# A hybrid decoder layer: the mixer's gates taken out of the pair loop into a second pass of seven-product blocks

## The chip, the core and the metric

The kernel runs on one core of a Trainium2 chip. The metric is device time in microseconds (us) of one execution; three runs of the kernel before gave 1593.44 us in the median (1592.82 to 1595.67). A profile is one further execution, recorded by the hardware profiler.

## What is computed

One decoder layer on x of 1024 tokens x 1024 channels, in float32. Cut to what matters:

```python
h = rms_norm(x, norm_mix)
xa, ga, q, f, v, g, m_a, m_b = split(h @ w_in)          # eight projections, 1024 x 1024 each
xa = causal_depthwise_conv(xa)
r, i = sigmoid(xa @ w_r + b_r), sigmoid(xa @ w_i + b_i)  # blocks of 256 channels
log_a = -8 * r * softplus(-lam)
hh = scan(exp(log_a), sqrt(-expm1(2 * log_a)) * (i * xa))   # linear recurrence over tokens
y_a = hh * gelu(ga)
o = rms_norm(hgrn2(silu(q), f_gate(f), v), hg_norm)         # 8 heads of 128, decayed linear attention
y = sigmoid(m_a) * y_a + sigmoid(m_b) * o * silu(g)
x = x + y @ w_out
x = x + square(relu(rms_norm(x, norm_mlp) @ w_up)) @ w_down
return rms_norm(x, norm_final)
```

## The kernel before

Every product is taken in three passes: an operand is split into a rounded high part (H, a cast on ScalarE, line 78) and the rest (L, a subtraction on VectorE, line 79), and `mm3` (lines 123 to 125) issues H x H, H x L and L x H into one PSUM bank. "One matmul" below is one of these three. The engines are called TensorE (PE), VectorE (DVE, `V` in the code), ScalarE (ACT, `A`), GpSimd (POOL, `G`) and SyncE (SP, whose queue issues nearly all DMAs in program order).

The tokens are worked in two halves c of T = 512. For each half, `first_norm(c)` normalizes four tiles of 128 rows, transposes them on TensorE and splits them into `hT`. Then come four pairs p of 256 channels (two heads, one rg block). A pair projects v (`project_v`), xa, q and f (`project_steps`: 8 steps of 6 matmuls of 128x512, 48 in all), convolves xa (`conv`), runs the gated recurrence (`rg_lru`, 24 matmuls, scheduled ahead by a raised priority, placed after the second step of f), and then the attention (`hgrn`). `hgrn` is a long chain on VectorE and ScalarE with small blocks of scores between (tiles `sc`, then `pk`, `pkv`, `po`). While that chain runs, TensorE works on the generator `gates`: the four projections g, mb, ga, ma of the same pair, 48 matmuls each, with their activations. `go(GO[i])` says how many of the generator's steps are issued before each block of scores; GO = (17, 5, 1, 1, 2). The pair's y goes, split, into SBUF. TensorE's instructions are kept in the order in which they are written (`pin`); the other engines' instructions are placed by the scheduler, each engine then running its own in order.

Between the halves stands `out_proj(0)` with `first_norm(1)` in its middle. After the second half comes `out_proj` of the second half, into which the second norm (`second_norm`) is woven, and then the MLP. The MLP uses a product of 2x2 blocks with seven products in place of eight: `PLAN` names, for each of the seven steps, a PSUM bank (X, Y or Z), a combination of weight blocks (A11, A12, A22, s1 to s4, made by `quad_steps`) and a combination of the four blocks of the activation (B11, B21, B22, t1, n2, T3, T4, made by `combos`). One such block of work is 84 matmuls of 128x512. Sixteen blocks are the up projection (uX, uY, uZ in the trace), sixteen the down projection (dX, dY, dZ).

Weight tiles come in `seq` order: `load_w` into one of 4 raw buffers (0.5 MB), `split_w` into two of 6 split buffers. `next_w` takes the next one and fills up to two ahead.

Of the kernel before, what the change touches and what calls it, by code (L numbers as in the profile page):

```python
# [18 lines left out]
P = 128  # L19
# [9 lines left out]
ORDER = ("v", "xa", "q", "f0", "rg", "f1", "g", "mb", "ga", "ma")  # L29
N_PAIR_TILES = 17  # L30
# [4 lines left out]
GO = (17, 5, 1, 1, 2)  # L35
# [8 lines left out]
def trunk(ctx: ExitStack, tc: tile.TileContext, x, wts, mlp, pv, gains, mask_f, mask_u, out):  # L44
# [12 lines left out]
    a2y, close_y = opened("a2y")  # L57
    a2h, close_h = opened("a2h")
# [5 lines left out]
    seq = []  # L64
    for c in range(NC):
        seq += list(range(MIX_TILES + OUT_TILES))
    seq += list(range(MIX_TILES, MIX_TILES + OUT_TILES))
# [16 lines left out]
    def load_w(i):  # L84
        raw = raw_tile(f"raw{i}")
        nc.sync.dma_start(raw, wts[i])
        return raw
# [10 lines left out]
    def fill_w(n):  # L98
        while made[0] < min(n, len(seq)):
            i = seq[made[0]]  # L100
# [48 lines left out]
    def transposed(xn, dst, tt, name):  # L149
        for h in range(2):  # L150
            pt = bank("hg", f"xT_{name}_{h}")
            for k in range(4):
                PE.transpose(pt[:, k * P : (k + 1) * P], xn[:, (4 * h + k) * P : (4 * h + k + 1) * P], ident)
# [3 lines left out]
    def a2_set(pool, name):  # L157
        return [
            [pool.tile([P, 4, T], F32R, tag="a2", name=f"{name}{q}{h}", bufs=4) for h in range(2)] for q in ("H", "L")
        ]  # L160
# [4 lines left out]
    xt_cm = tc.tile_pool(name="xt", bufs=2)  # L165
    xt_pool = xt_cm.__enter__()

    def tile_x(name):
        return xt_pool.tile([P, D], F32, tag="xt", name=name)

    x2d = [dram.tile([P, D], F32, tag=f"x2_{t}", name=f"x2_{t}") for t in range(8)]
# [3 lines left out]
    mix = tc.tile_pool(name="mix", bufs=1)  # L175
# [8 lines left out]
    def small_inputs():  # L184
        nc.sync.dma_start(pvt, pv)
        nc.sync.dma_start(mf, mask_f)
        mu32 = mt("kT", "mu32", (P, 4, P)).rearrange("p a b -> p (a b)")[:, : 7 * 32]
# [9 lines left out]
    t3, t4, t5, t6 = (par[:, i, :] for i in range(3, 7))  # L197

    def parameters():
# [27 lines left out]
        V.tensor_scalar(sp4, t3, 4.0, None, op0=ALU.mult)  # L227

# [10 lines left out]
    hT = []  # L239

    X_TAGS = ("g1", "g2", "on", "xc")

    def first_norm(c):
        dst = a2_set(a2h, f"hT{c}")
        xts = []
        for tt in range(4):
            r = c * 4 + tt
            xt = mt(X_TAGS[tt], f"x{r}", (P, D)) if c == 0 else tile_x(f"x{r}")
            nc.sync.dma_start(xt, x[r * P : (r + 1) * P, :])
            xts.append(xt)  # L250
            if c == 0 and tt == 0:
                gain0.append(gain_tile(0))
            if c == 0 and tt < 3:
                raws.append(load_w(seq[tt]))
        xns = {}

        def rows(tt):
            xns[tt] = mt("f" if tt % 2 == 0 else "tmp", f"xn{c}{tt}", (P, D))
            norm_rows(xts[tt], xns[tt], gain0[0], f"x{c}{tt}")

        def weights(n):
            if c == 0:
                fill_w(n)

        rows(0)
        weights(1)
        transposed(xns[0], dst, 0, f"x{c}0")
        rows(1)
        weights(2)
        for tt in range(1, 4):  # L270
            if tt < 3:
                rows(tt + 1)
            transposed(xns[tt], dst, tt, f"x{c}{tt}")
        weights(3)
        in_order[0] = False
        hT.append(dst)

    def project_steps(c, name):

        pp = [bank("pj", f"pj_{name}_{s}") for s in range(2)]  # L280
        for half in range(2):
            wh, wl = next_w()
            for k in range(4):
# [4 lines left out]
                yield  # L288
# [11 lines left out]
    def project(c, name):  # L300
        return run(project_steps(c, name))

    def project_v(c, name):
        v = mt("v", f"v_{name}", (P, 4, 256))
        w = [next_w(), next_w()]
        for tt in range(4):
            pp = bank("pj", f"pv_{name}_{tt}")
            for k in range(8):
# [4 lines left out]
                mm3(pp[:, :256], hh[:, cut], hl[:, cut], wh[:, cols], wl[:, cols], k == 0, k == 7)  # L313
            A.copy(v[:, tt, :], pp[:, :256])  # L314
        return v

    def conv(c, p, pp):
        xc = mt("xc", f"xc{c}{p}", (P, 2, T))
        for s in range(2):
            u = 2 * p + s  # L320
            xp = mt("xp", f"xp{c}{u}", (P, T + 16), bufs=2)
            V.tensor_copy(xp[:, 0:3], xcar[:, u, :])
# [7 lines left out]
            )  # L330
            for j in range(3):
# [15 lines left out]
    def rg_lru(c, p, xc, xh, xl):  # L347
        wh, wl = next_w()
        hs = mt("h", f"h{c}{p}", (P, 2, T))
        for s in range(2):  # L350
# [6 lines left out]
            w = mt("rw", f"rw{c}{u}")  # L357
            A.activation(w, pr, AF.Sigmoid, bias=pvt[:, PV_BR + u : PV_BR + u + 1])
            A.activation(w, w, AF.Tanh, scale=sp4[:, u : u + 1])
            ig = mt("ri", f"ri{c}{u}")  # L360
            A.activation(ig, pi, AF.Sigmoid, bias=pvt[:, PV_BI + u : PV_BI + u + 1])

            V.tensor_scalar(w, w, 0.0, None, op0=ALU.max)
            rec = mt("rr", f"rr{c}{u}")
            V.tensor_scalar(rec, w, 1.0, None, op0=ALU.add)
            V.reciprocal(rec, rec)  # L366
            A.activation(w, w, AF.Sqrt)
            V.tensor_tensor(out=ig, in0=ig, in1=xc[:, s, :], op=ALU.mult)
            V.scalar_tensor_tensor(w, w, 2.0, rec, op0=ALU.mult, op1=ALU.mult)
            V.tensor_tensor(out=ig, in0=ig, in1=w, op=ALU.mult)  # L370
            V.tensor_scalar(rec, rec, 2.0, -1.0, op0=ALU.mult, op1=ALU.add)
            h = hs[:, s, :]
            V.tensor_tensor_scan(h, rec, ig, hcar[:, u : u + 1], op0=ALU.mult, op1=ALU.add)
            if c + 1 < NC:
                G.tensor_copy(hcar[:, u : u + 1], h[:, T - 1 : T])
        return hs
# [25 lines left out]
    def hgrn(c, p, q1, f, kk, v, go):  # L402
# [90 lines left out]
        go(GO[0] - (OWN_BEFORE if c > 0 else 0))  # L493
# [71 lines left out]
        vn = lambda s, n: v[:, n, s * P : (s + 1) * P]  # L565
# [5 lines left out]
        kT = []  # L571
        for s, u in both:
            kT.append(mt(("kT", "rr")[s], f"kT{c}{u}", (P, 4, P)))
# [6 lines left out]
        states = []  # L580
        for s, u in both:
            sn = mt(("rw", "ri")[s], f"sn{c}{u}", (P, 4, P))
# [38 lines left out]
        return on  # L621

    def gates(c, p, got, dst):
        pg = yield from project_steps(c, f"g{c}{p}")
        g2 = mt("g2", f"g2{c}{p}", (P, 2, T))
        for s in range(2):
            A.activation(g2[:, s, :], pg[s], AF.Sigmoid)
            V.tensor_tensor(out=g2[:, s, :], in0=g2[:, s, :], in1=pg[s], op=ALU.mult)
        pb = yield from project_steps(c, f"mb{c}{p}")
        t = mt("tmp", f"smb{c}{p}", (P, 2, T))  # L630
        for s in range(2):
            A.activation(t[:, s, :], pb[s], AF.Sigmoid)  # L632
        V.tensor_tensor(out=g2, in0=g2, in1=t, op=ALU.mult)
        pa = yield from project_steps(c, f"ga{c}{p}")
        g1 = mt("g1", f"g1{c}{p}", (P, 2, T))
        t = mt("tmp", f"gel{c}{p}", (P, 2, T))
        for s in range(2):
            A.activation(t[:, s, :], pa[s], AF.Square)
            A.copy(g1[:, s, :], pa[s])
        V.tensor_scalar(t, t, 0.044715, 1.0, op0=ALU.mult, op1=ALU.add)  # L640
        V.tensor_tensor(out=t, in0=t, in1=g1, op=ALU.mult)
        A.activation(t, t, AF.Tanh, scale=GELU_C)
        V.scalar_tensor_tensor(g1, t, 1.0, g1, op0=ALU.add, op1=ALU.mult)
        pm = yield from project_steps(c, f"ma{c}{p}")
        for s in range(2):
            pt = bank("hg", f"poT{c}{p}{s}")
            for n in range(4):
                pin(PE.transpose(pt[:, n * P : (n + 1) * P], got["on"][:, 4 * s + n, :], ident))
            V.scalar_tensor_tensor(
                g2[:, s, :], pt, pvt[:, PV_HG : PV_HG + 1], g2[:, s, :], op0=ALU.mult, op1=ALU.mult  # L650
            )
        t = mt("tmp", f"sma{c}{p}", (P, 2, T))
        for s in range(2):
            A.activation(t[:, s, :], pm[s], AF.Sigmoid)
        V.scalar_tensor_tensor(g1, g1, 0.5, got["h"], op0=ALU.mult, op1=ALU.mult)
        for s in range(2):
            V.tensor_tensor(out=t[:, s, :], in0=g1[:, s, :], in1=t[:, s, :], op=ALU.mult)
            V.tensor_tensor(out=t[:, s, :], in0=t[:, s, :], in1=g2[:, s, :], op=ALU.add)
            split(t[:, s, :], *kt(dst, 2 * p + s))

    def out_proj(c, ys, res, done, between=lambda: None):
        for hf in range(2):
            pp = [bank("pj", f"po{c}{hf}{tt}") for tt in range(4)]
            for j in range(4):
                wh, wl = next_w()
                for k in range(2):
                    ku = 2 * j + k
                    yh, yl = kt(ys, ku)
# [8 lines left out]
            if hf == 0:  # L677
                between()

    def res0(tt, hf):  # L680
        xs = xt_pool.tile([P, 512], F32, tag="xs", name=f"xs{tt}{hf}", bufs=2)
# [6 lines left out]
    for c in range(NC):  # L688
        if c == 0:
            first_norm(0)  # L690
            mu32 = small_inputs()
        else:
            out_proj(0, ys, res0, done0, lambda: first_norm(1))
        ys = a2_set(a2y, f"y{c}")
# [20 lines left out]
    xt_cm.__exit__(None, None, None)  # L715
    close_h()

# [393 lines left out]
```

## Time and profile before

| | before |
|---|---|
| median of three runs | 1593.44 us (1592.82 to 1595.67) |
| the profiled execution | 1595.84 us, of which the span is 1594.0 us |
| PE busy | 1560.2 us, 98% of the span |
| DVE busy | 1206.5 us, 76% |
| ACT busy | 771.6 us, 48% |
| POOL busy | 64.9 us, 4% |
| granted TensorE clock, mean | 0.996 |
| moved by DMA | 246.51 MB, 155 GB/s in the mean |

The span runs from the first instruction to the last, and an engine's busy time is the part of it in which an instruction of its own runs. A matmul's duration in a row is longer than the distance to the next one, since they are pipelined. In rows of groups, `out<-in` gives the tiles' names with their numbers left out, then shapes, the count, busy time and mean ns, and after the last bar the idle time just before and what ended it. In rows of waits stand the waiting engine, tile and line, the releaser, and then total us, times and the longest. In rows of single instructions the start in us comes first, then the duration.

### The profile page before, as it was taken

How to read it: one execution, taken by the hardware profiler on the slowest of the kernel's cores; microseconds unless marked ns; L12 is line 12 of the kernel's file. 1: busy time of each engine (PE TensorE's matmuls, PEld its weight loads, DVE VectorE, ACT ScalarE, POOL GpSimd, SP SyncE). 2: the span in 40 equal slices, each digit the busy share in tenths (PEclk: the TensorE clock that was granted, in tenths of full speed). 3: DMA queues.
4: the chain of work that ended last, by engine and by line, in shares of the span. 5: the costliest groups of instructions: out<-in, count | busy, mean ns of one | idle time of the engine just before them, and what ended most of it. 6: DMA issues, size and time to landing. Idle time of an engine off the chain costs nothing.

```text
span 1594.0 us, 23215 instructions
## 1 busy us (share of the span) xinstructions
PE 1560.2 (98%) x9240; PEld 1305.6 (82%) x9240; DVE 1206.5 (76%) x1751; ACT 771.6 (48%) x1210; POOL 64.9 (4%) x107
## 2 busy tenths in 40 slices
PE   7999999999999999999999988999999999999997
PEld 6888898888888888888888866888888878888886
DVE  5985966958754865858759787988877888888877
ACT  4643545446433544546445576777667732221113
POOL 0010010100100010000100100000000000000000
PEclk9999999999999999999999998999999999999999
DMA  6212213222243213222222452766666565666652
GB/s 240 94 67 95 95 64 106 91 83 85 88 171 133 93 67 104 82 80 93 80 93 93 146 198 79 286 242 241 255 254 251 224 265 228 251 250 255 257 200 106
DMA packets 57996, 246.51 MB, mean 155 GB/s; under 512 B 6688, under 2 KB 6816, under 8 KB 47136
## 3 DMA queue, kind: packets, MB, share of 16 engines
q1 hardware_dynamic: 56304, 239.27, 40.3%
q10 hardware_dynamic: 1584, 5.77, 1.0%
q8 instruction: 72, 1.18, 0.3%
q14 instruction: 36, 0.29, 0.1%
HBM read 185.24 MB, written 59.77 MB: 154 GB/s over the span
## 4 chain that ended last, share of the span: by engine, by line
PE 66%; DVE 4%; DMA 1%; ACT 1%; issue 1%; POOL 0%; DVEq 0%; POOLq 0%; SPq 0%; ACTq 0%
PE dX L123 3%; PE uX L123 3%; PE dX L124 3%; PE dX L125 3%; PE uX L125 3%; PE uX L124 3%; PE uY L124 2%; PE uY L123 2%; PE uY L125 2%; PE po L124 2%; PE po L123 2%; PE po L125 2%; PE dY L123 2%; PE dY L124 2%; PE dY L125 2%; PE pj_ma L125 1%
## 5 line engine op out<-in xcount | busy, mean ns | idle before, releaser
L79 DVE TENSOR_TENSOR wL<-raw,wH 128x1024 fp32r<-128x1024 f32 x160 | 194.9, 1218 | 141.6 <-ACT wH L78 140.0
L78 ACT CAST wH<-raw 128x1024 fp32r<-128x1024 f32 x160 | 167.6, 1048 | 117.4 <-PE po L124 27.3
L1031 DVE TENSOR_TENSOR acc<-acc,dX 128x512 f32<-128x512 f32 x128 | 85.0, 683 | 29.4 <-PE dX L125 28.8
L78 ACT CAST wA<-q 128x512 fp32r<-128x512 f32 x32 | 19.8, 622 | 133.1 <-PE dX L125 101.5
L1031 DVE TENSOR_TENSOR acc<-acc,dY 128x512 f32<-128x512 f32 x64 | 43.4, 685 | 15.7 <-PE dY L125 14.5
L366 DVE RECIPROCAL rr<-rr 128x512 f32<-128x512 f32 x16 | 53.5, 3345 | 0.0
L891 ACT ACTIVATE b<-b 128x512 f32<-128x512 f32 x48 | 30.2, 630 | 37.1 <-DVE b L890 37.1
L123 PE MATMUL pv<-wH,hT0H 128*128 128x256 f32 x128 | 37.1, 290 | 0.2 <-ACT wH L78 0.2
L124 PE MATMUL pv<-wL,hT0H 128*128 128x256 f32 x128 | 36.7, 287 | 0.0
L125 PE MATMUL pv<-wH,hT0L 128*128 128x256 f32 x128 | 36.7, 287 | 0.0
L123 PE MATMUL pv<-wH,hT1H 128*128 128x256 f32 x128 | 36.5, 285 | 0.0
L124 PE MATMUL pv<-wL,hT1H 128*128 128x256 f32 x128 | 36.2, 283 | 0.0
L125 PE MATMUL pv<-wH,hT1L 128*128 128x256 f32 x128 | 36.2, 283 | 0.0
L332 DVE SCALAR_TENSOR_TENSOR xc<-xp,pvt,xc 128x512 f32<-128x512 f32 x48 | 33.1, 745 | 0.0
L892 ACT ACTIVATE b<-b 128x512 f32<-128x512 f32 x48 | 30.0, 630 | 1.1
L79 DVE TENSOR_TENSOR wA<-q,wA 128x512 fp32r<-128x512 f32 x32 | 22.0, 687 | 10.6 <-ACT wA L78 10.0
L511 ACT COPY kk<-kc 128x512 f32<-128x512 f32 x8 | 5.0, 622 | 45.1 <-DVE kc L405 45.1
L518 POOL TENSOR_SCALAR scT<-dd 32x256 f32<-32x256 f32 x32 | 23.1, 721 | 78.2 <-DVE dd L434 76.7
L123 PE MATMUL pj_ga<-hT1H,wH 128*128 128x512 f32 x64 | 26.2, 410 | 0.0
L123 PE MATMUL pj_ga<-hT0H,wH 128*128 128x512 f32 x64 | 26.2, 409 | 0.0
L314 ACT COPY v<-pv 128x256 f32<-128x256 f32 x32 | 11.8, 370 | 29.5 <-PE pv L125 29.5
L632 ACT ACTIVATE smb<-pj_mb 128x512 f32<-128x512 f32 x16 | 9.6, 599 | 34.1 <-PE pj_mb L125 34.1
(1861 smaller groups left out, 5252.4 us busy)
## 6 DMA issues: line engine op xcount, KB each, us to landing
raw<-wts_in SPq DMA_DIRECT2D x160, 512.0 KB, 3.4
q<-mlp_in SPq DMA_DIRECT2D x64, 512.0 KB, 4.0
x<-x_in SPq DMA_DIRECT2D x8, 512.0 KB, 6.4
acc<-x ACTq DMA_DIRECT2D x8, 512.0 KB, 6.3
y_out<-acc SPq DMA_DIRECT2D x16, 256.0 KB, 2.0
xs<-x_in SPq DMA_DIRECT2D x8, 256.0 KB, 3.4
x<-xs SPq DMA_DIRECT2D x8, 256.0 KB, 2.4
x2s<-x_in SPq DMA_DIRECT2D x4, 512.0 KB, 4.5
```

Source lines behind the costliest of these rows:

```text
L78: keep(A.copy(h, src))
L79: keep(V.tensor_tensor(out=lo, in0=src, in1=h.bitcast(F32), op=ALU.subtract))
L123: pin(PE.matmul(o, ah, bh, start=first, stop=False, **how))
L124: pin(PE.matmul(o, ah, bl, start=False, stop=False, **how))
L125: pin(PE.matmul(o, al, bh, start=False, stop=last, **how))
L314: A.copy(v[:, tt, :], pp[:, :256])
L332: V.scalar_tensor_tensor(xc[:, s, :], xp[:, j : j + T], pvt[:, PV_CW + 8 * j + u : PV_CW + 8 * j + u + 1], xc[:, s, :], op0=ALU.mult, op1= ...
L366: V.reciprocal(rec, rec)
L518: G.tensor_scalar(scT[32 * b : 32 * b + 32, :, 32 * b : 32 * b + 32], dd[32 * b : 32 * b + 32, :, :], 1.0, 0.0, op0=ALU.mult, op1=ALU.add,)
L891: A.activation(b[:, at, :], b[:, at, :], AF.Relu, scale=-1.0 if at == 2 else 1.0)
L892: A.activation(b[:, at, :], b[:, at, :], AF.Square)
L1031: V.tensor_tensor(out=dst, in0=dst, in1=banks[bk, pr], op=op)
```

## The change

The mixer is worked in two passes.

**Pass 1** runs over the eight (half, pair) items i. `hgrn(i)` is issued with a generator beside it as before, but the generator is now `stage(i + 1)`: v of item i, transposes of `on` of item i - 1 (`on_T`), then xa, the convolution, q, f and `rg_lru` of item i + 1. The h of the recurrence and the transposed `on` are written to memory (`hd`, `od`). The four row tiles of the second half are loaded, normalized and transposed inside the first four stages (`next_rows`). `rg_lru` takes its decay from an Exp on ScalarE instead of a reciprocal on VectorE, works on both 512-channel halves in one instruction where it can, and its ScalarE operations are chained in an order by hand. `make_combos(k)`, eight rounds written after the rg gate of stages 5 to 7, makes t1, n2, T3 and T4 of `hT` (six sums on POOL, two on VectorE, four splits) and writes them to memory (`cd`). The last stage projects v of the last item and g and mb of pair 0 plainly.

**Pass 2** computes the other 14 of 16 gate projections over both halves at once, each as one block of seven products (`gate_step`, 84 matmuls), with the gates' arithmetic in `gate_work`. It reads t1, n2, T4 and T3 back (eight loads of 1 MB), h and `on` pair by pair, and writes y, split, to memory. Then `out_proj(0)` and the rest follow as before.

```diff
-GO = (17, 5, 1, 1, 2)
+GO = (24, 5, 1, 1, 2)
...
+    def make_combos(i):
+        k, cut = i // 2, slice(256 * (i % 2), 256 * (i % 2) + 256)
+        r = tile_x(f"r{i}").rearrange("p (a b) -> p a b", a=4)
+        quarters = ((0, 0), (0, 1), (1, 1), (1, 0))
+        for j, (c, h) in enumerate(quarters):
+            hi, lo = (hT[c][q][h][:, k, cut].bitcast(F32) for q in range(2))
+            G.tensor_tensor(out=r[:, j, :], in0=hi, in1=lo, op=ALU.add)
+        b11, b21, b22, b12 = (r[:, j, :] for j in range(4))
+        G.tensor_tensor(out=b11, in0=b11, in1=b12, op=ALU.subtract)
+        G.tensor_tensor(out=b12, in0=b22, in1=b12, op=ALU.subtract)
+        V.scalar_tensor_tensor(b22, b11, -1.0, b22, op0=ALU.mult, op1=ALU.subtract)
+        V.scalar_tensor_tensor(b21, b22, -1.0, b21, op0=ALU.mult, op1=ALU.subtract)
+        for src, o in ((b11, "t1"), (b22, "n2"), (b12, "T3"), (b21, "T4")):
...
+            split(src, st[:, at, 0, :].bitcast(F32R), st[:, at, 1, :].bitcast(F32R))
+            nc.sync.dma_start(cd[o][:, :, k, cut], st[:, at])
...
-            rec = mt("rr", f"rr{c}{u}")
-            V.tensor_scalar(rec, w, 1.0, None, op0=ALU.add)
-            V.reciprocal(rec, rec)
-            A.activation(w, w, AF.Sqrt)
...
+        for s, u in us:
+            on_act(e[:, s, :], w[:, s, :], AF.Exp, scale=nsp8[:, u : u + 1])
+        for s, u in us:
+            on_act(w[:, s, :], w[:, s, :], AF.Tanh, scale=sp4[:, u : u + 1])
+        V.tensor_tensor(out=ig, in0=ig, in1=xc, op=ALU.mult)
+        V.tensor_scalar(w, w, 0.0, None, op0=ALU.max)
+        V.scalar_tensor_tensor(xc, e, 1.0, w, op0=ALU.add, op1=ALU.mult)
+        on_act(w, w, AF.Sqrt)
+        V.tensor_scalar(xc, xc, -1.0, 1.0, op0=ALU.mult, op1=ALU.add)
+        V.scalar_tensor_tensor(w, e, 1.0, w, op0=ALU.add, op1=ALU.mult)
+        V.tensor_tensor(out=ig, in0=ig, in1=w, op=ALU.mult)
...
+        nc.sync.dma_start(hd[p][:, 2 * c : 2 * c + 2, :], hs)
...
-        go(GO[0] - (OWN_BEFORE if c > 0 else 0))
+        go(GO[0] - 8 * (c + p == 0) - (OWN_BEFORE if c > 0 else 0))
...
+    def v_of(i):
+        def between(tt):
+            if tt == 0 and i > 1:
+                on_T(*where(i - 2), gots[i - 2])
+            if tt == 1 and "xn" in gots[i - 1]:
+                transposed(gots[i - 1]["xn"], hT[1], i - 1, f"x1{i - 1}")
+
+        yield from v_steps(*where(i - 1), gots[i - 1], between)
+
+    def stage(i):
+        c, p = where(i)
+        got = gots[i]
+        if i == 0:
+            yield from v_steps(c, p, got, lambda tt: None)
+        elif i > 1:
+            yield from v_of(i)
+        px = yield from project_steps(c, f"xa{c}{p}")
+        xc, xps = conv_in(c, p, px)
...
+        pq = yield from hooked(project_steps(c, f"q{c}{p}"), {} if i == 1 else {6: convolve})
+        got["q1"] = q_of(c, p, pq)
+        yield
+        fs = hooked(project_steps(c, f"f{c}{p}"), {6: convolve} if i == 1 else {})
+        for _ in range(2 if i != 1 else 7):
+            next(fs)
+            yield
...
+        yield from rg_lru(c, p, *got["xc"])
+        if i < 4:
+            got["xn"] = next_rows(i)
+        for k in {5: (0, 1, 2), 6: (3, 4, 5), 7: (6, 7)}.get(i, ()):
+            make_combos(k)
+        if i != 1:
+            pf = yield from fs
+            got["f"], got["kk"] = f_of(c, p, pf)
...
+    def last_stage():
+        yield from v_of(NC * NPAIR)
...
+        on_T(NC - 1, NPAIR - 1, gots[-1])
...
+    for i in range(NC * NPAIR):
+        rest = stage(i + 1) if i + 1 < NC * NPAIR else last_stage()
+        hgrn(*where(i), gots[i], lambda n: run(rest, n))
+        run(rest)
...
+    for o in ("t1", "n2", "T4", "T3"):
+        pool = np_ if o in ("t1", "n2") else tp
+        gop[o] = tuple(pool.tile([P, 4, T], F32R, tag=o + q, name=f"g{o}{q}") for q in "HL")
+        for q in range(2):
+            nc.sync.dma_start(gop[o][q].bitcast(F32), cd[o][:, q])
...
+    def gate_step(q, step):
+        bk, wo, ho = PLAN[step]
...
+        for k in range(4):
+            cols = slice(k * P, (k + 1) * P)
+            mm3(o, wh[:, cols], wl[:, cols], hh[:, k, :], hl[:, k, :], first and k == 0, k == 3, not first)
+        if step < 3:
+            ge[q, step] = gp.tile([P, T], F32, tag="e", name=f"ge{step}_{q}", bufs=4)
+            A.copy(ge[q, step], o)
+        elif step < 6:
+            at, e = {3: (0, 0), 4: (2, 1), 5: (3, 2)}[step]
+            V.tensor_tensor(out=b[:, at, :], in0=o, in1=ge.pop((q, e)), op=ALU.add)
+        else:
+            A.copy(b[:, 1, :], o)
...
+    own = list(range(2, QUADS))
+    for q in own[:2]:
+        load_quad(GQ + q)
+        gwork[q] = quad_steps(GQ + q, (w1p, wp))
+        gwork[q]["a"]()
+        if q == own[0]:
+            gwork[q]["sums"]()
+        gwork[q]["d"]()
+        gate_step(q, 0)
+        gate_step(q, 3)
+    gwork[own[0]]["b"]()
+    live["g2"] = gp_tile("b", "g2_0")
+    nc.sync.dma_start(live["g2"], g2d)
+    with_o(0)
+    for q in own:
...
+            if n == QUADS:
+                if step == 2:
+                    close_np()
+                    yp, close_yp = opened("yp", side="right")
+                    y_tiles(yp, 0)
...
+            if step == 1:
+                load_quad(GQ + n)
+            for k in {2: ("sums", "a", "b"), 5: ("c",), 6: ("d",)}.get(step, ()):
+                gwork[n][k]()
+        gate_work(q)
```

In the trace of the changed kernel the blocks of pass 2 are called gX, gY and gZ with the block's number, 2 to 15, its weights wA11, wA12, ws1 and ws3 with 32 added to the number, and the tiles of `make_combos` r0 to r7.

More of the change, by code (lines that the diff above doesn't have):

```diff
@@ L98, in fill_w @@
     def fill_w(n):
-        while made[0] < min(n, len(seq)):
-            i = seq[made[0]]
+        while made[0] < min(n, most[0]):
+            i = made[0]
             raw = raws.pop(0) if raws else load_w(i)
@@ L330, in conv @@
             )
+            xps.append(xp)
+        return xc, xps
+    def conv(c, p, xc, xps):
+        for s in range(2):
+            u = 2 * p + s
+            xp = xps[s]
+            V.tensor_copy(xp[:, 0:3], xcar[:, u, :])
             for j in range(3):
@@ L620, in hgrn @@
         mul(on, on, rs.unsqueeze(2).to_broadcast([P, 8, P]))
[L621 to L659, printed above, removed]
@@ L661, in out_proj, with hooked @@
-    def out_proj(c, ys, res, done, between=lambda: None):
+        got["on"] = on
+    gots = [{} for _ in range(NC * NPAIR)]
+    where = lambda i: divmod(i, NPAIR)
+    def hooked(steps, hooks):
+        n = 0
+        while True:
+            try:
+                next(steps)
+            except StopIteration as end:
+                return end.value
+            n += 1
+            if n in hooks:
+                hooks[n]()
+            yield
+    def v_of(i):
[5 more added lines that the diff above has]
+        yield from v_steps(*where(i - 1), gots[i - 1], between)
@@ new lines, in plain @@
+    def plain(c, w, name):
+        pp = [bank("pj", f"{name}{c}{s}") for s in range(2)]
+        for half in range(2):
+            wh, wl = w[half]
+            for k in range(4):
+                hh, hl = kt(hT[c], 4 * half + k)
+                for s in range(2):
+                    cols = slice(s * 512 + k * P, s * 512 + (k + 1) * P)
+                    mm3(pp[s], wh[:, cols], wl[:, cols], hh, hl, half == 0 and k == 0, half == 1 and k == 3)
+                if half == 0 or k < 3:
+                    yield
+        return pp
@@ new lines, in trunk, with gp_tile @@
+    GQ = 2 * QUADS
+    gwork, gb, gbank, ge, live = {}, {}, {}, {}, {}
+    SIGN = (1.0, -1.0, -1.0, 1.0)
+    def gp_tile(tag, name):
+        return gp.tile([P, 4, T], F32, tag=tag, name=name, bufs=4 if tag == "b" else 1)
+    def gate_step(q, step):
+        bk, wo, ho = PLAN[step]
+        first = (q, bk) not in gbank
+        if first:
+            gbank[q, bk] = bank(BANK[bk], f"g{bk}{q}")
+        if q not in gb:
+            gb[q] = gp_tile("b", f"gb{q}")
+        o, b = gbank[q, bk], gb[q]
+        wh, wl = ops_w[GQ + q][wo]
+        hh, hl = gop[ho]
+        for k in range(4):
+            cols = slice(k * P, (k + 1) * P)
[8 more added lines that the diff above has]
+            A.copy(b[:, 1, :], o)
@@ new lines, in with_o, with y_tiles, ykt @@
+    def with_o(p):
+        o = load_4(od[p], f"o{p}")
+        V.tensor_tensor(out=live["g2"], in0=live["g2"], in1=o, op=ALU.mult)
+    yt = {}
+    def y_tiles(pool, c):
+        yt[c] = [pool.tile([P, 2, 2, T], F32R, tag=f"y{p}", name=f"y{c}{p}") for p in range(NPAIR)]
+        for p in range(NPAIR - (c == 0)):
+            nc.sync.dma_start(yt[c][p].bitcast(F32), yd[p][:, :, 2 * c : 2 * c + 2, :])
+    def ykt(c, ku):
+        p, s = divmod(ku, 2)
+        t = yt[c][p]
+        s = s if c == 0 else 1 - s
+        return t[:, 0, s, :], t[:, 1, s, :]
@@ new lines, in trunk @@
+    own = list(range(2, QUADS))
[13 more added lines that the diff above has]
+    for q in own:
+        n = q + 1
+        if n > own[1] and n < QUADS:
+            gwork[n] = quad_steps(GQ + n, (w1p, wp))
+        for step in (0, 1, 2, 3, 4, 5, 6):
+            if q in own[:2] and step in (0, 3):
+                if q == own[0] and step == 3:
+                    gwork[q]["c"]()
+                    gwork[q + 1]["sums"]()
+                continue
+            gate_step(q, step)
+            if q == own[0]:
+                if step > 4:
+                    gwork[n]["b" if step == 5 else "c"]()
+                continue
+            if n == QUADS:
[3 more added lines that the diff above has]
+                    y_tiles(yp, 0)
+                    most[0] = len(seq)
+                    fill_w(n_mix + 1)
+                if step == 5:
+                    fill_w(n_mix + 3)
+                continue
+            if step == 1:
[3 more added lines that the diff above has]
+        gate_work(q)
```

403 lines of the change are left out of this document (265 added, 138 removed).

## The prediction, made before the change was run

> **What bounds the kernel now.** I read the page's first line and its chain first, then what TensorE waited for.
>
> ```profile
> PE 1560.2 (98%) x9240; PEld 1305.6 (82%) x9240; DVE 1206.5 (76%) x1751; ACT 771.6 (48%) x1210; POOL 64.9 (4%) x107
> PE 66%; DVE 4%; DMA 1%; ACT 1%; issue 1%; POOL 0%; DVEq 0%; POOLq 0%; SPq 0%; ACTq 0%
> PE xT_x L153 <- DVE xn L147: 10.3, 2, 9.4
> PE xT_h L772 <- DVE rstd_h L145: 6.2, 2, 5.6
> ```
>
> TensorE is busy for 98% of the span and carries the chain. Its two largest waits, 10.3 us at the start and 6.2 us in the second norm, lie in code that the change leaves nearly alone. So the kernel costs what its matmuls cost, until an edit makes them wait. What margin the others have, by stage:
>
> ```profile
> 155.72:259.99 104.27, 104.27 (x757) 89.25 (x756) 74.98 (x113) 50.80 (x86) 8.41 (x13) 1.00 0.25 87
> 1025.00:1075.00 50.00, 50.00 (x221) 41.17 (x220) 41.59 (x52) 35.38 (x51) 0.00 (x0) 1.00 0.66 253
> ```
>
> The columns are the stretch, its length, then busy time of PE, weight loads, DVE, ACT and POOL, the granted clock, the DMA share and GB/s. The first row is one pair of the mixer: PE 104.27 of 104.27, DVE 75. The second is 50 us of the MLP's seven-product blocks: PE 50.00 of 50, DVE 41.6 beside it. That second row matters, because the new second pass is made of such blocks: they run at TensorE's pace.
>
> **1. Fewer matmuls: -38.1 us.** The price of one comes from the distance of two starts 48 matmuls apart (the 389 ns in the second column overlap).
>
> ```profile
> 40.56 0.39 PE L123 MATMUL pj_q<-hT0H,wH 128*128 128x512 f32 x1
> 51.45 0.39 PE L123 MATMUL pj_f<-hT0H,wH 128*128 128x512 f32 x1
> ```
>
> 10.89 us / 48 = 0.2268 us. Before, four gates x 8 (pair, half) x 48 = 1536. After, 14 blocks of 7 products x 12 = 1176, and g and mb of pair 0 as plain projections, 192: together 1368. The difference is 168 x 0.2268 = 38.1 us, and nothing else on TensorE changes in number. It is taken where PE was at 100%, so it counts in full.
>
> **2. The stages of pass 1: +1 us.** A stage loses four gate projections, 4 x 10.89 = 43.6, and keeps 104.3 - 43.6 = 60.7 us of PE. VectorE loses this:
>
> ```profile
> L79 DVE TENSOR_TENSOR wL<-raw,wH 128x1024 fp32r<-128x1024 f32 x160 | 194.9, 1218 | 141.6 <-ACT wH L78 140.0
> L366 DVE RECIPROCAL rr<-rr 128x512 f32<-128x512 f32 x16 | 53.5, 3345 | 0.0
> L628 DVE TENSOR_TENSOR g<-g,pj_g 128x512 f32<-128x512 f32 x16 | 11.1, 694 | 0.0
> L658 DVE TENSOR_TENSOR sma<-sma,g 128x512 f32<-128x512 f32 x16 | 11.0, 685 | 0.3
> ```
>
> 8 weight splits x 1.22 = 9.7; 2 reciprocals x 3.35 = 6.7 (ScalarE's Exp takes their place); the gates' 13 operations between L628 and L658, 0.69 to 1.29 us each, about 11.3. That leaves 75 - 27.7 = 47 us; adding up the durations of what stays gives 52, so I take a slack of 9 to 13 us in a stage of 60.7. What must not be late is the score blocks:
>
> ```profile
> 195.26 0.89 PE L415 MATMUL sc<-q,kk 128*32 128x48 f32 x64
> 195.81 0.69 DVE L405 TENSOR_TENSOR qb<-qb,seg 128x512 f32<-128x512 f32 x1
> 196.65 0.89 PE L415 MATMUL sc<-qb,kc 128*32 128x48 f32 x64
> ```
>
> The last operand was ready at 196.5, as the third block began at 196.65: exactly balanced now. f's 48 matmuls from 155.72 and the rg gate's 24 among them end at 172.0, so 23 us of other matmuls cover the chain. After, v, the transposes, xa and half of q stand there, about 24 us, against a VectorE chain of 22.5 to 24 without the gates' splits. The second half's norms, until now inside out_proj(0), move into the first four stages: a square on ScalarE, a power on POOL and about 2.6 us on VectorE for each row tile lie in the slack, and the wait that they caused goes (10.3 - 9.4 = 0.9 in the row of the first norm). I put +1 us in all for eight stages; bounds -1 and +6. The stores of h and on, 0.5 MB each, go into SP's queue beside a DMA share of 0.25 and delay no load by more than 1.2 us, which the weights' lead of two tiles covers.
>
> **3. The sums for the second pass (make_combos): +23 us.** They are written in the last three stages, but in the built program's order five of the eight rounds, r2 to r6, stand together in the stage of the first half's pair 3, with r1 ahead and r7 behind. A round is 6 sums of 128x256 on POOL, one after the other, then 2 on VectorE that wait for them, 4 casts on ScalarE and 4 subtractions on VectorE. The sums' tile has one buffer, so round n+1 on POOL waits until round n is split, and VectorE, in order, waits for POOL in every round: nothing overlaps. No POOL tensor sum of this size is in the trace; the nearest rows are:
>
> ```profile
> L518 POOL TENSOR_SCALAR scT<-dd 32x256 f32<-32x256 f32 x32 | 23.1, 721 | 78.2 <-DVE dd L434 76.7
> L608 POOL COPY scar<-sn 128x128 f32<-128x128 f32 x8 | 4.5, 585 | 21.4 <-DVE sn L589 21.4
> L463 POOL TENSOR_SCALAR seg<-seg 128x128 f32<-128x128 f32 x8 | 3.5, 431 | 317.8 <-DVE seg L405 317.8
> L405 DVE TENSOR_TENSOR qb<-qa,seg 128x256 f32<-128x256 f32 x24 | 9.5, 433 | 0.0
> ```
>
> I take 0.72 (the row with 256 elements per partition): 6 x 0.72 + 0.3 of handoffs = 4.6, and 6 x 0.43 = 2.6 on VectorE, 7.2 us a round. Five rounds hold VectorE for 36 us, of which one stage's slack, 13, hides a part: 36 - 13 = 23. Followed through the queues, about 17 us of it fall into that stage and 6 into the next: POOL's copies into scT stand behind the sums, ScalarE's casts wait for POOL ahead of the rg gate's evictions and weight casts, and VectorE's weight splits and the next score chain stand behind both, so PE waits at scores, states, the rg gate and the next weights. With 0.43 (128x128, half the size) it is 5 x 5.5 - 13 = 14; with 1.0 (the copy's 585 scaled up) 5 x 8.9 - 13 = 31; and 10 if VectorE spends part of the wait where it is idle today.
>
> The Trainium skill (GPSIMD Engine Reference, section 3.1) gives 2.6 cycles an element for a two-input sum, which I estimate at 0.6 us here; the sum would be 5 x 6.5 - 13 = 19 instead of 23. No run here shows that yet.
>
> **4. Between the passes: +20 us.** SP's queue is in order. After the last transposes of pass 1, ScalarE writes the last onT, and its store stands in SP's queue ahead of the eight 1 MB loads of t1, n2, T4 and T3; behind those stands the second half of the second block's weights (q351, 0.5 MB). TensorE's order after the transposes is 36 matmuls that need none of it (gZ2, gX2, gX3: 8.2 us), then gZ3, which needs q351 cast and subtracted. 8.4 + 0.5 = 8.9 MB at the best rate that the trace shows:
>
> ```profile
> 8.00:10.00 2.00, 0.57 (x3) 0.57 (x4) 1.91 (x2) 0.53 (x1) 0.06 (x1) 1.00 1.02 418
> L78 ACT CAST wH<-raw 128x1024 fp32r<-128x1024 f32 x160 | 167.6, 1048 | 117.4 <-PE po L124 27.3
> raw<-wts_in SPq DMA_DIRECT2D x160, 512.0 KB, 3.4
> ```
>
> 8.9 MB / 418 GB/s = 21.3 us; with about 1.5 for the store's issue and ScalarE ahead, 2 of latency (3.4 for 0.5 MB, less the 1.2 that its bytes take) and the 1.05 cast, 26. Less the 8.2 of cover: 18. And a wait of this length costs more behind it:
>
> ```profile
> 953.20:958.75 5.55, 0.00 (x0) 0.03 (x1) 5.07 (x10) 3.72 (x7) 0.86 (x1) 0.98 0.59 240
> 960.00:962.00 2.00, 1.55 (x8) 1.18 (x7) 2.00 (x3) 1.97 (x4) 0.00 (x0) 0.50 0.73 258
> ```
>
> After 5.55 us without a matmul the granted clock was still 0.50 at 960 to 962; half of about 4 us is lost, 2. Sum 20, bounds 5 (the loads start earlier than SP's order lets me see) and 26 (253 GB/s, as the MLP's row moves, for part of it).
>
> **5. The second pass and what follows: +1 us.** A block is 84 matmuls, 19 us; beside it VectorE has 4 sums, 7 weight subtractions, 3 evictions and the gate's work, not more than the 83% of the MLP row. y comes back from memory before out_proj(0), under the last block's matmuls. Start-up is as before. I put 1 us, bounds 0 and 6.
>
> **The sum.** -38.1 + 1 + 23 + 20 + 1 = +6.9. The profiled execution took 1595.84 us (its span of 1594.0 and 1.84 around it), so 1602.7 by it; that execution lies 2.4 above the median of the runs, 1593.44, against which I forecast **1600**.
>
> **The rivals.**
> - *VectorE catches up with the sums* (faster). It has 9 to 13 us of slack in the next stages too; if PE's operands of the stage are all made before the rounds, only a few us remain. With 5 us in place of 23: 1593.4 - 38.1 + 1 + 5 + 20 + 1 = 1582; with the loads hidden too, 1567. It decides from where the sums cost less than 13 us: below that the kernel is faster by over 3. For it: VectorE is idle 29 of 104 us today. Against: the rounds' strict alternation, and POOL and ScalarE held too.
> - *The loads are hidden* (faster): if the 8.9 MB are not served in the order of the queue and q351 lands early, about 5 of the 20 stay: 1585. Against it: one queue, q1, moved 239 of the 247 MB.
> - *Everything waits for POOL* (slower still): sums at 1.0 us, 31, loads 24, and the eight stages late by 6: 1593.4 - 38.1 + 6 + 31 + 24 + 3 = 1619. Its mechanism would be POOL and VectorE slowing each other; the rows of POOL, at most 8% busy, can't show it. The Trainium skill (GPSIMD Engine Reference, section 1) says the two share their interfaces to SBUF, with contention where a VectorE instruction has two SBUF inputs, which speaks against this change; no row here shows its price.
>
> **Chances.** Forecast, 1591 to 1609: 0.42. Sums hidden: 0.23. Loads hidden: 0.10. All wait for POOL: 0.20. Left over: 0.05. A measurement of this kernel can tell about 0.2%, 3.2 us, from no change. Faster by more: both faster rivals whole and a little of the forecast, 0.35; within 0.2%: 0.06; slower: 0.59. The range reaches from 1572, between the two values of the first rival, to 1620, the slower rival's own time; it leaves out about half of that rival and the corner where both costs vanish.
>
> **What would show it.** Step 1: matmuls 168 fewer, and the second pass at PE 100% with blocks of 19 us. Step 3: in the stage of pair 3 of the first half, VectorE and POOL alternating at about 7 us a round, PE idle by some 17 us there and 6 in the next; wrong, if VectorE's rounds lie in PE-busy time. Step 4: one PE wait of about 18 us ended by the split of the second block's weights, and a clock of 0.50 behind it; wrong, if it is under 5. Step 2 is wrong if PE waits for VectorE by over 1 us in each stage. The whole is wrong if the gates' pass itself runs below PE's pace.

## The result, and the profile after

The changed kernel takes **1623.37 us** in the median of four runs (1621.82 to 1623.72), the kernel before 1594.09 beside it (four runs, 1592.82 to 1595.67): 1.0181 times as long, 95% interval 1.0164 to 1.0199. It is slower, as forecast, but by 29 us where the working had 7, and 3 us beyond the range.

The first line of the page, the chain and the longest waits of TensorE, in the changed kernel:

```profile
PE 1540.3 (95%) x9072; PEld 1285.3 (79%) x9072; DVE 1217.1 (75%) x1778; ACT 810.9 (50%) x1277; POOL 125.4 (8%) x155
PE 77%; DVE 12%; DMA 3%; ACT 3%; POOL 3%; issue 2%; DVEq 0%; POOLq 0%; SPq 0%; ACTq 0%
PE gZ L132 <- ACT wA1235H L87: 17.3, 1, 17.3
PE xT_x L162 <- DVE xn L156: 10.1, 2, 9.4
PE xT_h L1097 <- DVE rstd_h L154: 6.2, 1, 6.2
PE xT_h L1097 <- DVE xn_h L156: 5.9, 5, 2.4
PE sc L613 <- DVE qb L485: 5.1, 2, 3.0
PE pk L650 <- DVE kk L485: 4.3, 3, 2.6
```

x9240 has become x9072: the 168 matmuls are gone. Yet PE's busy time fell by 1560.2 - 1540.3 = 19.9 us, not by 38.1. The other 18 us are longer matmuls, most of them behind waits, at a granted clock of 0.50, as the rows further down show. To that come waits that were not there: the one of 17.3 us for q351, and many of 1 to 3.5 us in pass 1, ended by VectorE or ScalarE.

Where the time lies: five stages of pass 1 (from one pkv block to the next), columns as in the prediction:

```profile
106.50:163.00 56.50, 53.31 (x525) 45.96 (x524) 48.38 (x86) 34.00 (x67) 17.44 (x21) 0.97 0.31 104
163.00:225.90 62.90, 62.12 (x573) 54.02 (x572) 49.37 (x88) 40.92 (x74) 11.49 (x13) 1.00 0.31 102
225.90:296.70 70.80, 64.04 (x574) 55.26 (x573) 51.31 (x94) 41.11 (x77) 24.72 (x24) 0.98 0.33 105
296.70:377.80 81.10, 66.97 (x564) 56.69 (x563) 58.89 (x115) 43.81 (x88) 33.05 (x42) 0.94 0.41 137
377.80:438.70 60.90, 60.90 (x564) 53.04 (x563) 46.93 (x81) 37.17 (x66) 6.07 (x7) 1.00 0.35 113
```

A stage without rounds of sums takes 60.9 us at PE 100%, as worked out. The fourth row, with five rounds in it (r3 to r7), takes 81.1, and its matmuls are busy 67.0 us for the same 564 that take 60.9 in the fifth: there is idle time, and there is slow time, at a mean clock of 0.94.

Two marks that both kernels have, the first matmul of n2 in the up projection (before, then after) and the first of the output projections:

```profile
L123 PE MATMUL uX<-h2n2H,ws10H x4: 389/389/389, 980.5 to 982.5; 128*128 128x512 f32 x4
L123 PE MATMUL po<-wH,y1H x64: 388/389/477, 901.3 to 952.3; 128*128 128x512 f32 x64
```

```profile
L132 PE MATMUL uX<-h2n2H,ws10H x4: 389/389/389, 1009.4 to 1011.4; 128*128 128x512 f32 x4
L132 PE MATMUL po<-wH,y x128: 388/389/628, 881.6 to 978.8; 128*128 128x512 f32 x128
```

The first mark comes 28.9 us later, so all of the loss stands ahead of it, and the MLP is unchanged. From out_proj to that mark: 1009.4 - 881.6 = 127.8 us after; before, 79.2 and the 43.5 of out_proj(0)'s 192 matmuls, 122.7. The last 5 us of the loss are in the second norm.

### The profile page after: what moved, and what is told of

Read it like the earlier page. It is cut to its first block, busy times and chain, and to the rows that moved or that the text cites. A ratio compares the mean times of both kernels' runs of the same rounds, so it can differ in the third digit from the quotient of the medians.

```text
span 1621.8 us, 23129 instructions
## 1 busy us (share of the span) xinstructions
PE 1540.3 (95%) x9072; PEld 1285.3 (79%) x9072; DVE 1217.1 (75%) x1778; ACT 810.9 (50%) x1277; POOL 125.4 (8%) x155
## 4 chain that ended last, share of the span: by engine, by line
PE 77%; DVE 12%; DMA 3%; ACT 3%; POOL 3%; issue 2%; DVEq 0%; POOLq 0%; SPq 0%; ACTq 0%
PE dX L132 4%; PE dX L133 3%; PE dX L134 3%; PE uX L132 3%; PE uX L134 3%; PE uX L133 3%; PE gX L132 3%; PE gX L133 3%; PE gX L134 3%; PE dY L132 2%; PE dY L134 2%; PE dY L133 2%; PE gY L132 2%; PE uY L134 2%; PE gY L133 2%
## 5 line engine op out<-in xcount | busy, mean ns | idle before, releaser
L88 DVE TENSOR_TENSOR wL<-raw,wH 128x1024 fp32r<-128x1024 f32 x100 | 121.8, 1220 | 64.7 <-ACT wH L87 63.1
L87 ACT CAST wH<-raw 128x1024 fp32r<-128x1024 f32 x100 | 104.7, 1050 | 78.4 <-PE po L133 27.0
L1310 DVE TENSOR_TENSOR acc<-acc,dX 128x512 f32<-128x512 f32 x128 | 84.9, 682 | 29.4 <-PE dX L134 28.8
L1310 DVE TENSOR_TENSOR acc<-acc,dY 128x512 f32<-128x512 f32 x64 | 43.5, 685 | 15.8 <-PE dY L134 14.5
L133 PE MATMUL po<-wL,y 128*128 128x512 f32 x128 | 50.4, 393 | 0.0
L134 PE MATMUL po<-wH,y 128*128 128x512 f32 x128 | 50.2, 392 | 0.0
L132 PE MATMUL po<-wH,y 128*128 128x512 f32 x128 | 50.1, 391 | 0.0
L876 DVE TENSOR_TENSOR s<-s,q 128x512 f32<-128x512 f32 x46 | 31.5, 686 | 0.6
L875 DVE TENSOR_TENSOR s<-q,q 128x512 f32<-128x512 f32 x46 | 31.5, 687 | 0.5
L877 DVE TENSOR_TENSOR s<-q 128x512 f32<-128x512 f32 x46 | 31.6, 686 | 0.5
L878 DVE TENSOR_TENSOR s<-s,q 128x512 f32<-128x512 f32 x46 | 31.5, 684 | 0.2
L133 PEld LDWEIGHTS po<-wL,y 128*128 128x128 f32 x128 | 24.3, 190 | 4.9
L685 PE MATMUL po<-v,scT 128*128 128x128 f32 x128 | 24.6, 286 | 3.8 <-DVE sn L671 3.8
L132 PEld LDWEIGHTS po<-wH,y 128*128 128x128 f32 x128 | 24.2, 189 | 5.0
```

Source lines behind the costliest of these rows:

```text
L87: keep(A.copy(h, src))
L88: keep(V.tensor_tensor(out=lo, in0=src, in1=h.bitcast(F32), op=ALU.subtract))
L132: pin(PE.matmul(o, ah, bh, start=first, stop=False, **how))
L133: pin(PE.matmul(o, ah, bl, start=False, stop=False, **how))
L134: pin(PE.matmul(o, al, bh, start=False, stop=last, **how))
L875: V.tensor_tensor(out=sa[:, 0, :], in0=a21, in1=a22, op=ALU.add)
```

## The experiments

The ratios are to runs of the kernel before on the same chip, times are medians, and "less" is against the changed kernel's 1623.37 us, whose own interval is about 3 us to either side.

**e1: no rounds of sums.**

```diff
-        for k in {5: (0, 1, 2), 6: (3, 4, 5), 7: (6, 7)}.get(i, ()):
-            make_combos(k)
...
-            nc.sync.dma_start(gop[o][q].bitcast(F32), cd[o][:, q])
+            nc.sync.dma_start(gop[o][q].bitcast(F32), next(stand))
```

> The rounds of make_combos are left out, and the eight loads between the passes read h and on in place of t1, n2, T4 and T3 (so pass 2 works on wrong operands, with the same instructions and the same 8.4 MB). Theory 1 (the eight rounds hold VectorE, POOL and ScalarE up in order, and TensorE's waits and the half clock behind them come from that): of the 36.6 us lost in pass 1 about 34 go, 1589 us (1585 to 1594). Rival 2 (the loss lies in the stages themselves: second half's norms and transposes woven in, v and the transposes of on beside the attention chain): at least 1612.

1593.71 us (ratio to before 0.999, 0.9981 to 0.9999): 29.7 less than the changed kernel, where the theory had 34. The kernel leaves the sums out, so its second pass works on other operands. The same stages in its trace:

```profile
106.30:160.40 54.10, 51.60 (x526) 44.93 (x526) 48.06 (x84) 34.00 (x67) 13.49 (x16) 1.00 0.34 108
160.40:223.30 62.90, 62.13 (x574) 54.03 (x573) 48.46 (x84) 39.56 (x70) 7.83 (x12) 1.00 0.28 93
223.30:287.40 64.10, 62.22 (x574) 54.04 (x573) 48.78 (x84) 38.73 (x69) 9.58 (x13) 1.00 0.28 91
287.40:348.20 60.80, 60.80 (x564) 52.97 (x563) 46.31 (x81) 37.03 (x66) 10.10 (x9) 1.00 0.29 96
```

Row by row against the four stages above, PE's idle time falls by 0.7, 0, 4.9 and 14.1 (19.7 us), and its busy time, for the same work, by 1.7, 0, 1.8 and 6.2 (9.7 us). So the rounds cost 29.4: two thirds waiting, one third longer matmuls, in the rows in which the clock is below 1.00. What remains in these rows, 2.5, 0.8 and 1.9 us of idle time, belongs to the stages themselves. Rival 2 is out.

**e2: the sums on VectorE.**

```diff
-            G.tensor_tensor(out=r[:, j, :], in0=hi, in1=lo, op=ALU.add)
+            V.tensor_tensor(out=r[:, j, :], in0=hi, in1=lo, op=ALU.add)
...
-        G.tensor_tensor(out=b11, in0=b11, in1=b12, op=ALU.subtract)
-        G.tensor_tensor(out=b12, in0=b22, in1=b12, op=ALU.subtract)
+        V.tensor_tensor(out=b11, in0=b11, in1=b12, op=ALU.subtract)
+        V.tensor_tensor(out=b12, in0=b22, in1=b12, op=ALU.subtract)
```

> The six sums of a round run on VectorE instead of POOL; the places are the scheduler's. If VectorE's waiting for POOL is what costs (Theory 1, alternation), a round falls from about 7.2 us of held VectorE to 12 x 0.43 = 5.2 with no wait, and about a third of the loss in pass 1 goes: 1611 (1605 to 1617). If it is the work on VectorE that costs (rival 3), 2.6 us a round more work: 1623 to 1640.

1599.71 us (1.0032, 1.0022 to 1.0042): 23.7 less, twice what was expected. The wait that has gone, as the changed kernel's trace shows it on POOL and on VectorE (start, duration, in brackets the idle time before and what ended it):

```profile
302.92 0.72 POOL L312 TENSOR_TENSOR r<-r 128x256 f32<-128x256 f32 x1
...
308.82 0.72 POOL L309 TENSOR_TENSOR r<-hT00H,hT00L 128x256 f32<-128x256 f32 x1 [2.06 <-DVE stT L88]
```

```profile
303.67 0.48 DVE L313 SCALAR_TENSOR_TENSOR r<-r 128x256 f32<-128x256 f32 x1 [4.05 <-POOL r L312]
304.07 0.33 DVE L671 SCALAR_TENSOR_TENSOR sn<-sn,seg,pkv 128x128 f32<-128x128 f32 x1
...
322.89 0.42 DVE L313 SCALAR_TENSOR_TENSOR r<-r 128x256 f32<-128x256 f32 x1 [4.63 <-POOL r L312]
```

```profile
DVE r L313 <- POOL r L312: 25.8, 6, 4.6
PE po L685 <- DVE sn L671: 3.8, 2, 3.5
```

VectorE stands at L313 for four to five us while the state update sn, ready to run, waits behind it, and TensorE's po waits for sn. In sum VectorE stood 25.8 us at that line, in six of the rounds. With the sums on VectorE it has more to do in the fullest stage (122 operations, where e1 has 81) and no such wait, and the clock stays up:

```profile
223.90:288.70 64.80, 62.43 (x573) 53.95 (x572) 52.81 (x98) 40.27 (x73) 12.85 (x12) 1.00 0.34 110
288.70:353.60 64.90, 61.53 (x564) 53.10 (x563) 60.07 (x122) 40.74 (x79) 12.38 (x11) 1.00 0.43 143
353.60:416.30 62.70, 61.49 (x563) 52.85 (x562) 57.82 (x112) 40.95 (x79) 9.02 (x9) 1.00 0.44 143
```

VectorE is busy 60.07 of 64.9 us and costs TensorE only a few us a stage. Rival 3 is out: it was not the work but the waiting, in order, for another engine. The scheduler also spread the rounds differently here (one, none, one, three and three in the five stages, where the changed kernel has five in one), so e2 alone does not separate the two; e3, which spreads them and keeps the sums on POOL, does.

**e3: the sums placed by hand.** Rounds two a stage in the last four; POOL's sums ordered behind its copies into scT, VectorE's first step of a round behind the evictions of q.

```diff
+            after(G.tensor_tensor(out=r[:, j, :], in0=hi, in1=lo, op=ALU.add), last_scT[0])
...
+        after(V.scalar_tensor_tensor(b22, b11, -1.0, b22, op0=ALU.mult, op1=ALU.subtract), last_q[0])
...
+            if i >= 4 and n < 2:
+                make_combos(2 * (i - 4) + n)
```

> Same rounds on the same engines, but two a stage in the four stages of the second half, ordered behind POOL's copies into scT and, on VectorE, behind the evictions of q, where VectorE was idle for about 8 of 10 us in the trace of after (444 to 454). Theory 1: nearly all of the loss goes, 1592 (1588 to 1600). Rival 2: at least 1612. Rival 3 (VectorE has no room for the rounds anywhere): 1605 to 1620.

1621.01 us (1.0161, 1.0146 to 1.0176): a miss, 2.4 less instead of 31, and not clear of the noise. Its stages say how: the crowded ones are gone, and each of the four later ones takes 67 to 68.5 us instead of 60.9. Two of them, and the longest waits between 300 and 580 us:

```profile
289.40:357.90 68.50, 61.60 (x563) 52.73 (x562) 50.86 (x93) 39.50 (x74) 18.45 (x21) 1.00 0.35 116
357.90:424.90 67.00, 61.57 (x564) 52.93 (x563) 51.04 (x92) 40.45 (x76) 18.52 (x20) 1.00 0.36 118
```

```profile
DVE r L320 <- POOL r L319: 16.9, 4, 4.6
DVE stt L88 <- ACT stt L87: 11.9, 5, 3.7
PE pr L132 <- ACT rw L427: 9.7, 4, 3.5
PE po L692 <- DVE sn L678: 7.9, 3, 2.6
```

(Its lines past 310 are 7 higher.) On VectorE I had tied down the two sums only. The splits of t1 and T3, which need nothing but POOL's sums, were still put ahead of sn (363.35, with 3.69 us of idle time, ended by ScalarE's cast), and the casts ahead of the rg gate's ScalarE work. In the whole run VectorE waited 33.7 us for the rounds (16.9 at L320, 16.8 at the splits), half of it at another line. Spreading the rounds did not lower their price here, where they still stood ahead of the attention chain in VectorE's queue and of the rg gate in ScalarE's.

**e4: q351 ahead.** The code of the eight loads is moved behind the first two blocks' first steps, so that SP issues q351 behind the first of them; T3 comes before T4.

```diff
-    for o in ("t1", "n2", "T4", "T3"):
-        pool = np_ if o in ("t1", "n2") else tp
...
     gwork[own[0]]["b"]()
+    for o in ("t1", "n2", "T3", "T4"):
+        pool = np_ if o in ("t1", "n2") else tp
```

> Between the passes the load of the second block's weights (q351) goes to SP's queue behind the first of the eight loads instead of behind the eighth, and T3 is loaded before T4. If the order of the queue sets the 17.3 us wait: the wait falls to 0 to 3 us, the half clock behind it goes, other waits for n2 and T3 of up to 4 us come: 1605 (1601 to 1609). Rival: the eight loads are needed just as soon by the steps behind gZ3, and the wait only moves: 1615 to 1623.

1611.53 us (1.0103, 1.0088 to 1.0118): 11.8 less, between the two. The long wait is 1.6 us now; n2's first product comes at 609.1 instead of 626.7, 17.6 us earlier. But a part comes back behind it, as the rival had it: new waits in the third block, where VectorE works without a gap from 629 to 645 on the late gate work of the first.

```profile
PE gX L134 <- DVE wA L88: 2.3, 1, 2.3
PE gZ L132 <- ACT onT L372: 1.9, 1, 1.9
PE gZ L132 <- ACT wA1235H L87: 1.6, 1, 1.6
PE gY L134 <- DVE ws136L L88: 1.1, 1, 1.1
```

**e5: e2 and e4 together.**

> The two edits together: sums on VectorE and q351 ahead of seven of the eight loads. They lie in different stages, so if the costs add up: 1623.4 - 23.7 - 11.8 = 1588 (1585 to 1591), faster than before by 0.4%. Rival: VectorE, fuller in both places, is late for the weights of the first blocks in pass 2: 1593 to 1600.

1588.80 us (0.9965, 0.9953 to 0.9978): the two add up, and the kernel is faster than the one before.

**e6: work in the wait.**

```diff
+        if (q, step) == (3, 3):
+            fh = ops_w[GQ + 2][wo][0]
+            for n in range(76):
+                tc.keep_in_program_order(PE.matmul(o, fh[:, :P], hh[:, n % 4, :], start=True, stop=True))
+        pinned[0] = (q, step) in ((2, 3), (2, 0), (3, 0), (3, 3))
...
```

The last line keeps TensorE's first four steps of pass 2 in their written order.

> 76 added matmuls of 128x512 (17.2 us at full clock) into the bank of gZ3 ahead of its own, on operands that are there, so that TensorE works through the wait for q351; their sums are thrown away by the first true matmul. If the wait without work is what halves the clock: PE wait for q351 0 to 1 us, granted clock 1.00 behind it in place of 0.50, and the time falls by the 2 to 2.5 us that gZ3 now loses: 1621 (1619.5 to 1622.5). If the clock falls for another reason (the loads' 426 GB/s): 0.50 stays and the added matmuls push the end out: 1627 to 1642.

1624.73 us (1.0197, 1.0182 to 1.0212), no gain. The clock did what was expected. First the changed kernel, the wait and the stretches behind it, then this one (the added matmuls and what follows them):

```profile
603.00:618.00 15.00, 0.00 (x0) 0.00 (x0) 0.00 (x0) 0.23 (x1) 0.00 (x0) 0.60 1.01 427
619.00:621.00 2.00, 1.96 (x4) 1.14 (x5) 2.00 (x2) 0.77 (x1) 0.00 (x0) 0.50 1.01 426
```

```profile
602.50:619.50 17.00, 17.00 (x77) 14.08 (x75) 0.00 (x0) 0.93 (x2) 0.00 (x0) 1.00 1.02 427
619.50:624.00 4.50, 3.91 (x16) 2.56 (x15) 3.69 (x4) 1.65 (x2) 0.00 (x0) 1.00 0.41 173
```

The same loads at 427 GB/s, and a clock of 1.00 with work, of 0.50 behind the wait without: at this place it is the idle time that halves it. TensorE reached t1's product 2.7 us earlier (621.2 against 623.9) and lost that again by n2's (626.4 against 626.7) and the mark (1009.4 in both). So at this place the half clock was hidden behind the weight splits that follow q351's, and the 2 us that the prediction put for it were not to be had.

**e7: the second norm from x.**

```diff
-            nc.sync.dma_start(xs, x2d[t])
+            nc.sync.dma_start(xs, x[t * P : (t + 1) * P, :])
```

> The second norm's first-half rows are read from x instead of from what out_proj(0) has just stored, so the mixer's part of those four row tiles is left out of the MLP's input; the loads stay. If the 5 us more of the second norm come from out_proj(0) now standing directly ahead of it (store, then load, of the same rows): the two waits of 2.4 us at 943 and 952 and the half clock behind go, 1618 (1616 to 1620). If they come from the weights' and y's loads in SP's queue: no change, 1622 to 1625.

1620.74 us (1.0167, 1.0151 to 1.0182): 2.6 less, not clear of the noise, with the wait for xn_h still 5.0 us in place of 5.9. Mostly a miss. So the rows that a norm reads are at most a small part of what it waited for. The waits of SP's queue in the changed kernel, from 915 to 960, show another candidate (L1111 is the second norm's first load):

```profile
SPq L1111 <- DMA x<-xs: 3.4, 1, 3.4
```

**e8: xs at the other end of SBUF.** The tiles of the second norm lay where out_proj(0)'s xs had been, so their loads, and all behind them in SP's queue, waited until the stores of xs were done.

```diff
-    xsp, close_xs = opened("xs")
+    xsp, close_xs = opened("xs", side="right")
```

> The changed kernel with one edit: the tiles xs of out_proj(0) lie at the other end of SBUF, so that the tiles of the second norm no longer take their place, and SP issues the norm's first loads before the last stores of xs are done (in after SP stood 3.4 us for those stores, ahead of the loads). If that wait is what makes the second norm 5 us dearer than before: 1619 (1617 to 1621). If out_proj(0)'s place makes it dearer otherwise (weights and stores in SP's queue): 1622 to 1625.

1617.85 us (1.0146, 1.013 to 1.0162): 5.5 less. From out_proj(0)'s first matmul (883.6) to the mark (1007.2) it takes 123.6 us in place of 127.8; before, the same work takes 122.7. In e1 to e6, whose xs lie as in the changed kernel, it takes 125.6 to 128.0. So the place of a buffer was worth 2 to 4 of the 5 us.

**e9: e2, e4 and e8 together.**

> Sums on VectorE, q351 early, and xs at the other end. If the three add up: 1588.8 less 2 to 4: 1585 (1583 to 1588), 0.6% faster than before. Rival: the norm is bound by its chain, no gain: 1588 to 1590.

1586.72 us (0.9952, 0.994 to 0.9965), 7.6 less than the kernel before and the fastest of all. Against e5 it is 2.1 less, with intervals that overlap; but from out_proj(0) to the mark it takes 122.4 us, as the kernel before does, and e5 takes 125.9. Its page and its longest waits:

```profile
PE 1529.5 (97%) x9072; PEld 1274.4 (80%) x9072; DVE 1232.8 (78%) x1826; ACT 809.9 (51%) x1277; POOL 92.4 (6%) x107
PE xT_x L162 <- DVE xn L156: 10.4, 2, 9.4
PE xT_h L1097 <- DVE rstd_h L154: 6.2, 2, 5.6
```

The two that lead now are those that led in the kernel before. PE's busy time is 30.7 us below the kernel before's, of the 38.1 that the matmuls are worth.

## Why the prediction was wrong in size

| step | forecast | measured | how |
|---|---|---|---|
| 1 fewer matmuls | -38.1 | -38.1 | 168 fewer; a steady stage at 60.9 us |
| 2 stages of pass 1 | +1 | about +7 | what is left of the 28.9; 5.2 of it idle time in e1's rows |
| 3 sums | +23 | +29.4 | changed kernel less e1, stage by stage |
| 4 between the passes | +20 | +23.4 | 591.5 to 623.9 less 48 matmuls, and 1.9 before |
| 5 second pass and after | +1 | +7 | 1.9 in pass 2, 5.1 in the second norm |
| sum | +6.9 | +28.9 | first mark |

The forecast sum was 22 us short: 6.4 of it lie in step 3, 6 each in steps 2 and 5, and 3.4 in step 4. Slower was right, and so was where the time would go; the sizes were not.

**Step 1** held. The blocks of pass 2 run at PE 100% at 19 us each, and the mechanism of the whole, 38 us less work and its gain spent on waits, was right.

**Step 3** named the mechanism: a sum on POOL took 0.73 us (0.72 was taken), and the waits were 19.7 us (23 forecast). That the two came so near is in part luck. The stage with five rounds, r3 to r7, lost 14.1 us (17 forecast), the one behind it nothing (6 forecast), and the one ahead, with r1 and r2, 4.9. The rounds began about 9.6 us apart or more (299.21, 308.82, 318.40), not 7. The Trainium skill's page (GPSIMD Engine Reference, section 3.1) had led to 0.6, and the measurement decides for 0.73. What failed is a term put at nothing without a reason: the 9.7 us of longer matmuls in these stages, at half clock behind some of the waits, which step 4 counted for the one long wait and step 3 for none. The first round, r0, was also not where I put it at no cost: VectorE stood 4.6 us for it at 146.9 in the stage of pair 1, and that stage lost 2.4 us more than e1's.

**Step 4** was right: one wait of 17.3 us (18 forecast), ended by the cast of wA1235H, a clock of 0.50 behind it. A wait of 1.9 us for the last onT ahead of gZ2, itself with a half clock behind, came on top. That q351's place in SP's queue sets the wait is shown by e4 (1.6 us); that not all of it comes back, too.

**Step 5** failed in a place that it passed over with "what follows". out_proj(0), which ended some 400 us ahead of the second norm before, now stands directly ahead of it, and the place of its buffers was not yet free: about +5 us, of which e8 gives back 2 to 4.

**Step 2** was 1 us beyond its bound of +6. About 2.5 us of it is idle time in the stage of pair 1, which is the only one without v as cover. What the other 2 of the 7 us are was not settled.

**The rivals.** "VectorE catches up" decided on the sums costing less than 13 us; they cost 29. The reason given against it, that the rounds alternate strictly and hold POOL and ScalarE too, is what e2 and e3 show together. "Everything waits for POOL" came out nearest, at 1619, with another make-up: the sums were as fast as POOL's rows said (two of 48 took 1.6 and 3.6 us), and VectorE's weight split takes 1220 ns in the changed kernel, 1218 before, so the contention that the Trainium skill states (GPSIMD Engine Reference, section 1) isn't needed for the result.

## What to carry to other kernels

Before work is handed to an idle engine, look at what stands behind the instruction that will wait for it: in a queue that runs in order, a round trip to POOL costs its whole length to everything behind it, and doing the six sums on the busy engine itself was 24 us cheaper. Price a wait of TensorE with the slow time that can stand behind it, short waits included. Where a step comes to stand next to another, look at the buffers and the DMA queue that they share, not only at the engines.

## What the runs showed of the hardware

TensorE's clock fell to half after some waits of 2.3 to 3.5 us, not only after long ones. Three places in the changed kernel, behind idle times of 2.3 us (ahead of 148.6), 3.5 (306.4) and 2.6 (374.2):

```profile
148.00:152.00 4.00, 3.42 (x8) 2.72 (x9) 4.00 (x8) 0.00 (x0) 1.05 (x1) 0.59 0.57 146
308.00:310.00 2.00, 2.00 (x10) 1.94 (x10) 0.67 (x3) 0.41 (x2) 1.18 (x2) 0.50 0.90 338
374.00:376.00 2.00, 1.78 (x8) 1.71 (x9) 2.00 (x5) 0.87 (x2) 1.88 (x3) 0.50 0.62 227
```

The length of a wait alone does not decide it. In the same trace a wait of 2.4 us (ahead of 945.14) was followed by 3.5 us at 1.00, another of 2.4 us (ahead of 954.56) by 3.1 us at 0.50. Two waits of 3.52 us, in the changed kernel and in e3:

```profile
306.45 1.23 PE L685 MATMUL po<-v,scT 128*128 128x128 f32 x4 [3.52 <-DVE sn L671]
307.34 0.50 PE L132 MATMUL pr<-xcH,wH 128*128 128x512 f32 x1 [3.52 <-ACT rw L427]
```

Behind the first the clock was 0.50 for the next 3.5 us, behind the second 1.00. What decides between them was not tried.

Ahead of the shortest of the three stood 2.2 us of score blocks, 48 columns wide. The Trainium skill (TensorE: Matmul & The Clock Gate, Part 1) gives an idle window of about 3.4 us, which runs freely, for this; here idle times shorter than that were enough at some places, and whether the light blocks ahead of them count as idle was not tried.

Two small POOL operations inside seg became longer, with no change to them: the one of 128x32 took 0.25 us in the mean before and 1.79 after (0.75 in e1), the one of 128x128 took 0.43 and 1.08 (1.80 in e1). VectorE waited for them 0.3 us in all in the changed kernel and 0.9 in e1. The cause stays open; that POOL and VectorE slow each other there was not ruled out.
